# Decoder step on one core: token sums by VectorE instead of GpSimd, and an earlier index search with the later jobs planned behind it

## The chip, the cores and the metric

The kernel runs on one core of a Trainium2 chip. The metric is device time in microseconds for one launch; the time before is the median of three runs, and one more execution was taken by the hardware profiler. The engines are named as the profile names them: PE (TensorE, its matrix multiplications), PEld (TensorE, loading of stationary operands), DVE (VectorE), ACT (ScalarE), POOL (GpSimd) and SP (SyncE, which only issues DMAs here). Engines run their own queues in order, each with its waits, and meet through semaphores.

## The reference

One decoder layer on a prompt of 1024 tokens and on 8 sample sequences of one token each, all in float32. The token vector (2048 wide) is normalised, multiplied by one wide matrix, split into heads, and two branches are computed: sparse attention and an mLSTM. Their outputs are gated, concatenated and multiplied by an output matrix.

```
h = rmsnorm(x, norm_w); p = split(h @ w_in)
scores = sum_h relu(q_idx[h] . k_idx) * w_idx[h]      # "indexer", 16 heads of 64
idx = top_k(scores, 256)                              # causal, per query
o   = softmax(q . k[idx] * scale) . v[idx]            # 8 heads, 2 KV heads
C, n, m, h_ml = mlstm(mq, mk, mv, igate, fgate)       # chunks of 64
x   = x + concat(o * silu(az), norm(h_ml) * sigmoid(mo) * silu(mz)) @ w_out
y   = rmsnorm(x, final_norm_w)
```

For the 8 samples keys and values come from a paged cache of 4096 positions, are scored, the best 256 are selected, and the rows are gathered.

## The kernel before, in words

**Precision.** Every large float32 product is made of three matmuls: each operand is split into a high part (H, a cast by ACT) and a low part (L, the remainder, a subtraction by DVE), and H·H, H·L and L·H are added in PSUM. So each new operand costs one ACT and one DVE instruction before PE can use it. L256/L257 are such splits of weights, L1676/L1677 of token sums.

**Stages on PE.** (1) The projection: tiles t = 0 to 20 of 128 weight columns (L1547), in three chunks of 344 tokens, 144 matmuls a tile. (2) The gate stage: tiles 21 to 60, made with fewer products out of sums of weight blocks and sums of token blocks, in the manner of Strassen. Each product is 48 matmuls of 128x258 (L1729) into PSUM tiles `pj`. Its phases are: phase 0, 20 pairs of products, which in the order of product matmuls is from 2640 to 4560; phase 1, to 5520, with the token sum in slot 1; phase 3, to 6480, slot 0; phase 2, slot 2; and the rest to 9360. In phase 0 a fourth PSUM tile, `extra`, is taken out of the pool of 5 banks (`bank`) that the side jobs use for their matmuls. After each half product DVE evacuates PSUM with a combine (L1824). (3) The output projection (L2094).

**Token sums.** `job_prep` makes them in 16 steps: X (two halves of a token block, 128x516 each) is loaded through the DMA queue of POOL (L1402), multiplied by the norm weight (L1412) and by the reciprocal root mean square (L1413), four sums and differences are formed (L1418 to L1421), and the results are stored to `xsD` (L1422, L1423). X has 3 buffers, O (three sums) has 1; loads go out two steps ahead. In the gate stage `fill(slot, op)` puts eight loads of a sum into a list; each `tick`, once per half product, issues one of them, and three ticks later its split (L1676 on ACT, L1677 on DVE). `pin` keeps an instruction in the order in which it is written.

**Weight sums.** `job_usum` sums weight blocks by DMAs that add in memory (L1435, L1439).

**Side jobs.** All other work is written as generators that yield a weight, in three lanes. A job has a start and an end in tiles, and after every tile or half product `Lane.step` runs the lane's current job until its share of weight up to the end is used. Lane 0: gates, index, att, ml. Lane 1: prep, dscore, dsel, qrows, datt (which waits for the index to be done), dml. Lane 2: usum. `T_AK` is 9 and `T_G` is 21. A scheduler with a model of time then fixes each engine's queue from this order, the priorities and the pins.

**The index.** `job_index` treats query blocks in three groups of two. A load brings a quad (four heads of a query block; `qi`, L450, on ACT's queue). For each head PE makes the scores (L468), ACT applies relu (L470), DVE weights and adds them (L473). Then a binary search for the 256th score runs in steps of ACT sign counts (L517) and DVE counts (L543). For the samples `dscore` and `dsel` do the same: L1062, L1083, L1089 and L1079 on DVE, L1064 on PE, whose total L1087 reads. `datt` then gathers keys (L1294), forms logits on DVE (L1318, L1322), transposes (L1336), makes a softmax (L1341 to L1351, PE L1358, L1359), multiplies gathered values (L1372) and writes out (L1379). `att` does the prompt's attention: transposes L597, logits L634, L635 on DVE, exponentials L651 on ACT, transposes L678, values L687.

```
def step(self, now, amount=1.0):        # Lane
    self.now = now
    self.debt -= amount
    while self.debt < 0:
        ...
        self.debt += self._next()       # weight * (quarter tiles left to end) / weight left
```

## Time and profile before

| | before |
|---|---|
| median of 3 runs | 2004.84 us (2001.0 to 2009.59) |
| profiled execution | 1996.96 us |
| its span | 1995.2 us |
| mean granted PE clock | 0.976 |
| PE busy | 1903.5 us |
| DVE busy | 1391.9 us |
| ACT busy | 916.5 us |
| POOL busy | 516.5 us |
| moved by DMA | 474.46 MB |

The profiled execution lies 0.4% under the median of the runs. Times in the trace are counted from the start of the span. Product matmuls follow one another on PE, so their count is a clock of its own: product matmul 2640 ends at 518.5 us, 4560 at 784.5 us, 5520 at 976.5 us, 6480 at 1185.7 us, 9360 at 1644.2 us.

### The profile page before, as it was taken

How to read it: one execution, taken by the hardware profiler on the slowest of the kernel's cores; microseconds unless marked ns; L12 is line 12 of the kernel's file. 1: busy time of each engine (PE TensorE's matmuls, PEld its weight loads, DVE VectorE, ACT ScalarE, POOL GpSimd, SP SyncE). 2: the span in 40 equal slices, each digit the busy share in tenths (PEclk: the TensorE clock that was granted, in tenths of full speed). 3: DMA queues.
4: the chain of work that ended last, by engine and by line, in shares of the span. 5: the costliest groups of instructions: out<-in, count | busy, mean ns of one | idle time of the engine just before them, and what ended most of it. 6: DMA issues, size and time to landing. Idle time of an engine off the chain costs nothing. (4 is left out here: it accounts for less than half of the span.)

```text
span 1995.2 us, 37381 instructions
## 1 busy us (share of the span) xinstructions
PE 1903.5 (95%) x13422; PEld 1822.9 (91%) x13422; DVE 1391.9 (70%) x3261; ACT 916.5 (46%) x1826; POOL 516.5 (26%) x614
## 2 busy tenths in 40 slices
PE   9999989999999999995699999999999999999997
PEld 9999989999999999994599989999999999977876
DVE  8554245765698988976465656566897666788887
ACT  8222136345434466410355545545565434455645
POOL 0698921222111000034000111011112131106633
PEclk9999999999999999897799999999999999999999
DMA  7578674665998647597577999678898957898866
GB/s 258 172 217 242 210 205 143 196 178 160 312 311 259 181 149 238 184 336 256 128 198 226 290 290 277 181 223 270 299 331 294 224 198 255 273 344 285 291 207 221
DMA packets 252918, 474.46 MB, mean 238 GB/s; under 512 B 40549, under 2 KB 116133, under 8 KB 246333
## 3 DMA queue, kind: packets, MB, share of 16 engines
q1 hardware_dynamic: 217261, 356.70, 54.6%
q0 software_dynamic: 21504, 107.32, 21.2%
q10 hardware_dynamic: 13968, 8.06, 1.4%
q8 instruction: 105, 1.72, 0.3%
q14 instruction: 80, 0.66, 0.1%
HBM read 381.54 MB, written 174.32 MB: 279 GB/s over the span
## 5 line engine op out<-in xcount | busy, mean ns | idle before, releaser
L1729 PE MATMUL pj<-xH 128*128 128x258 f32 x1920 | 545.5, 286 | 6.1 <-ACT xH L1676 2.8
L1729 PE MATMUL pj<-xL,xH 128*128 128x258 f32 x1920 | 547.0, 285 | 0.3 <-DVE xL L1677 0.2
L1729 PE MATMUL pj<-xH,xL 128*128 128x258 f32 x1920 | 545.9, 285 | 0.0
L1729 PEld LDWEIGHTS pj<-xH 128*128 128x128 f32 x1920 | 363.9, 190 | 9.5 <-ACT xH L1676 3.8
L1729 PEld LDWEIGHTS pj<-xL,xH 128*128 128x128 f32 x1920 | 365.6, 190 | 2.5 <-DVE xL L1677 0.9
L1729 PEld LDWEIGHTS pj<-xH,xL 128*128 128x128 f32 x1920 | 365.4, 191 | 1.5
L1547 PE MATMUL pj<-xH,wH 128*128 128x344 f32 (+1 forms) x816 | 265.4, 328 | 0.9 <-DVE mfull L379 0.5
L1547 PE MATMUL pj<-xL,wH 128*128 128x344 f32 (+1 forms) x816 | 265.0, 325 | 0.0
L1547 PE MATMUL pj<-xH,wL 128*128 128x344 f32 (+1 forms) x816 | 264.8, 325 | 0.0
L1439 POOL DMA_DIRECT2D usD<-in_wa_dram x80 | 65.9, 892 | 604.4 <-DMA usD<-in_wa_dram 367.9
L257 DVE TENSOR_TENSOR wL<-wraw,wH 128x512 fp32r<-128x512 f32 (+2 forms) x151 | 116.8, 784 | 120.5 <-ACT wH L256 111.3
L256 ACT CAST wH<-wraw 128x512 fp32r<-128x512 f32 (+2 forms) x151 | 90.0, 608 | 216.9 <-PE pj L1547 151.4
L1547 PEld LDWEIGHTS pj<-xH,wH 128*128 128x128 f32 x816 | 153.8, 189 | 2.1 <-ACT xH L313 0.9
L1547 PEld LDWEIGHTS pj<-xL,wH 128*128 128x128 f32 x816 | 154.0, 189 | 0.8 <-DVE xL L314 0.3
L1547 PEld LDWEIGHTS pj<-xH,wL 128*128 128x128 f32 x816 | 154.0, 189 | 0.3
L2094 PE MATMUL pj<-wH,sH 128*128 128x512 f32 x336 | 131.0, 390 | 0.7 <-ACT wH L2078 0.4
L2094 PE MATMUL pj<-wL,sH 128*128 128x512 f32 x336 | 125.9, 392 | 5.3 <-DVE wL L2083 5.0
L2094 PE MATMUL pj<-wH,sL 128*128 128x512 f32 x336 | 130.7, 389 | 0.0
L470 ACT ACTIVATE rl<-bank 128x512 f32<-128x512 f32 (+2 forms) x160 | 79.1, 522 | 90.7 <-PE bank L468 50.7
L473 DVE SCALAR_TENSOR_TENSOR s<-rl,wiN,s 128x512 f32<-128x512 f32 (+2 forms) x150 | 95.0, 653 | 31.7 <-ACT rl L470 29.5
L1729 PE MATMUL bank<-xL,xH 128*128 128x258 f32 x320 | 91.4, 286 | 0.0
L1729 PE MATMUL bank<-xH,xL 128*128 128x258 f32 x320 | 91.3, 285 | 0.0
(487 smaller groups left out, 4466.7 us busy)
## 6 DMA issues: line engine op xcount, KB each, us to landing
usD<-in_wa_dram POOLq DMA_DIRECT2D x80, 512.0 KB, 8.0
wraw<-in_wt_dram SPq DMA_DIRECT2D x144, 256.0 KB
usD<-in_wa_dram SPq DMA_DIRECT2D x40, 512.0 KB
usD<-usD POOLq DMA_DIRECT2D x40, 512.0 KB, 7.2
wraw<-in_wa_dram SPq DMA_DIRECT2D x78, 256.0 KB
wraw<-in_wo_dram SPq DMA_DIRECT2D x64, 256.0 KB
ev<-spD SPq DMA_DIRECT2D x62, 258.0 KB
spD<-ev SPq DMA_DIRECT2D x60, 258.0 KB
```

What stands on the lines that cost most here:

```text
L256: a = SC.copy(H[:, s, :cols], raw[:, s, :cols])
L257: return a, V.tensor_tensor(L[:, s, :cols], raw[:, s, :cols], H[:, s, :cols].bitcast(F32), OP.subtract)
L470: SC.activation(r[:, :cn], p[:, :cn], AF.Relu)
L473: v = V.scalar_tensor_tensor(s[:, c0:c0 + cn], r[:, :cn], wv, s[:, c0:c0 + cn], OP.mult, OP.add)
L1439: pin(G.dma_start(usD[n, i], src, accum_op=OP.add, max_dma_last_dim=8192))
L1547: m = PE.matmul(ps[:cols, :cn], w_[:, k, :cols], x_[kk][:, c0:c0 + cn], start=(kk == ends[0] and z == 0), stop=(kk == ends[1] and z == 2))
L1729: PE.matmul(ps[c], w_[:, q, ks], x[y][:, c * CS:c * CS + CS], start=(first and q == 0 and k == 0 and z == 0), stop=(q == 1 and k == 3 and ...
L2094: PE.matmul(ps[b], S_[x][:, b * 128:b * 128 + 128], T_[y], start=(k == 0 and z == 0), stop=(k == 7 and z == 2))
```

## The change

1. *Token sums.* The multiplications by weight and by rms become one fused DVE instruction for each half (two a step), and the four POOL sums become three DVE instructions, the first of which makes two sums at once. The order of the sums in `xsD` changes, and with it the numbers in `fill`. The DMAs stay on POOL's queue.
2. *Index.* `qi` has 3 buffers, three quads are loaded at the start and after each search, later loads are two quads ahead. The job stands from tile 9.6 to 26.5 (12.3 to 30 before).
3. *Plan.* The start and end of prep, dscore, dsel, qrows, datt, att, ml, dml and usum are moved.
4. *Gate stage.* The slot splits are written at high priority, and the fill of slot 1 starts 20 half products into phase 0 instead of 40.

```diff
@@ job_index
-                    qis[n] = px.tile([128, 4, 128], F32R, name="qi", bufs=2)
+                    qis[n] = px.tile([128, 4, 128], F32R, name="qi", bufs=3)
...
-            load_q(0)
-            load_q(1)
+            for n in range(3):
+                load_q(n)
...
-                            if nq + 1 < len(quads) and (nq + 1) % 8 > 1:
-                                load_q(nq + 1)
+                            if (nq + 2) % 8 > 2:
+                                load_q(nq + 2)
...
-                load_q(nq)
-                load_q(nq + 1)
+                for z in range(3):
+                    load_q(nq + z)
@@ job_prep
-                a11, a21, a12, a22 = (X[:, y, h] for y in range(2) for h in range(2))
                 for y in (1, 0):
-                    w = nw[:, k + 8 * y:k + 8 * y + 1].unsqueeze(2).to_broadcast([128, 2, CS])
-                    pin(G.tensor_tensor(X[:, y], X[:, y], w, OP.mult))
-                    pin(G.tensor_tensor(X[:, y], X[:, y], halves[:, :, c:c + CS], OP.mult))
+                    pin(V.scalar_tensor_tensor(X[:, y], X[:, y], nw[:, k + 8 * y:k + 8 * y + 1], halves[:, :, c:c + CS],
+                                               OP.mult, OP.mult))
...
-                pin(G.tensor_tensor(O[:, 0], a21, a22, OP.subtract))
-                pin(G.tensor_tensor(O[:, 2], a11, a21, OP.subtract))
-                pin(G.tensor_tensor(O[:, 1], O[:, 0], a11, OP.subtract))
-                pin(G.tensor_tensor(a12, a12, O[:, 1], OP.add))
+                pin(V.tensor_tensor(O[:, 0:2], X[:, 0], X[:, :, 1], OP.subtract))
+                pin(V.tensor_tensor(O[:, 2], O[:, 1], X[:, 0, 0], OP.subtract))
+                pin(V.tensor_tensor(X[:, 1, 0], X[:, 1, 0], O[:, 2], OP.add))
@@ lanes
-                   Job("index", T_AK + 3.3, 30, ...),
-                   Job("att", T_G, 45.0, ...),
-                   Job("ml", T_G + 20, 56.6, ...)]),
-             Lane([Job("prep", 3, T_AK + 4.2, ...),
-                   Job("dscore", T_AK + 6, 21.0, ...),
-                   Job("dsel", T_AK, 28.5, ...),
-                   Job("qrows", T_G + 0.2, 29, ...),
-                   Job("datt", T_G + 4, 32.0, ...),
-                   Job("dml", T_G + 20, 54.5, ...)]),
-             Lane([Job("usum", T_AK + 3.4, 46.0, ...)])]
+                   Job("index", T_AK + 0.6, 26.5, ...),
+                   Job("att", T_G + 8, 44.5, ...),
+                   Job("ml", T_G + 20, 57.0, ...)]),
+             Lane([Job("prep", 3, T_AK + 2, ...),
+                   Job("dscore", T_AK + 3, 18.0, ...),
+                   Job("dsel", T_AK, 26.0, ...),
+                   Job("qrows", T_G + 0.2, 27, ...),
+                   Job("datt", T_G + 7.5, 32.5, ...),
+                   Job("dml", T_G + 20, 55.0, ...)]),
+             Lane([Job("usum", T_AK + 3.0, 46.0, ...)])]
@@ gate_stage
-                pin(SC.copy(h, l.bitcast(F32)))
-                pin(V.tensor_tensor(l, l.bitcast(F32), h.bitcast(F32), OP.subtract))
+                with tc.high_priority():
+                    pin(SC.copy(h, l.bitcast(F32)))
+                    pin(V.tensor_tensor(l, l.bitcast(F32), h.bitcast(F32), OP.subtract))
...
-        fills += [None] * (NP * 2)
-        fill(1, 3)
+        fills += [None] * NP
+        fill(1, 4)
...
-        fill(0, 4)
+        fill(0, 2)
...
-        fill(1, 2)
+        fill(1, 3)
```

In the changed file lines behind 1424 are numbered 2 or 3 lower: L1729 becomes L1727, L1824 becomes L1822, L1713 and L1718 (splits of weights for the products) become L1711 and L1716. Three places of the engines' order show what moves.

PE at the end of phase 1, before: the rows are the last matmuls of phase 1 (L1729), then those of `datt` and `att`.

```order
L1729 MATMUL pj_5145<-xL,xH 128x258
L1729 MATMUL pj_5145<-xH,xL 128x258
L1336 MATMUL bank<-cst,lT 64x128
L1338 MATMUL bank<-onesf,kn 64x1
L1336 MATMUL bank<-cst,lT 64x128
L1358 MATMUL bank<-cst,jk 128x64 x2
L1359 MATMUL bank<-cst,pb 128x64
L1372 MATMUL bank<-cv,PZ 32x256 x16
L1379 MATMUL bank<-cst,jk 128x128 x4
L597 MATMUL bank<-cst,pP 128x128 x8
L634 MATMUL bank<-xH,qH 128x512
```

They stand together behind product matmul 5520; the first matmul of phase 3 follows only after L634 and L678. In the changed kernel the same matmuls stand among those of phase 1. The first of them, on PE, behind product matmul 5059:

```order
L1727 MATMUL pj_5635<-xH 128x258
L1336 MATMUL bank<-cst,lT 64x128
L1338 MATMUL bank<-onesf,kn 64x1
L1727 MATMUL pj_5635<-xL,xH 128x258
L1727 MATMUL pj_5635<-xH,xL 128x258
L1727 MATMUL pj_5635<-xH 128x258
L1727 MATMUL pj_5635<-xL,xH 128x258
L1727 MATMUL pj_5635<-xH,xL 128x258
L1336 MATMUL bank<-cst,lT 64x128
L1727 MATMUL pj_5633<-xH 128x258
```

The others follow at product matmuls 5108 (L1358), 5149 to 5282 (L1372), 5308 (L1379), 5432 (L597) and 5458 (L634). The index's first score (L468) stands at product matmul 1056, where before it stood at 1452, and its last at 2933, before at 3937.

PE in the changed kernel in phase 0, behind product matmul 2808 (its row comes first): a run of index scores (L468) and of dsel's totals (L1064), of which rows are left out in two places.

```order
L1727 MATMUL pj_5635<-xH,xL 128x258
L468 MATMUL bank<-ki_1987,qi 128x384
L468 MATMUL bank<-ki_1988,qi 128x384
L468 MATMUL bank<-ki_1987,qi 128x512
L468 MATMUL bank<-ki_1988,qi 128x512
...
L1064 LDWEIGHTS onesb
L1064 MATMUL bank<-cb,onesb 128x24
L468 MATMUL bank<-ki_1987,qi 128x512
L468 MATMUL bank<-ki_1988,qi 128x512
...
L1727 MATMUL bank<-xH 128x258
```

In all 58 matmuls L468 and four L1064 stand there without a product between; before, they lay between products. The matmul that follows writes `extra`, in a PSUM bank that a total of dsel had last.

DVE in the changed kernel, early in the projection: the fused passes (L1410) and sums (L1416 to L1418) of prep stand in DVE's queue between its other work.

```order
L257 TENSOR_TENSOR wL<-wraw,wH 128x512
L1410 SCALAR_TENSOR_TENSOR X<-X,nw,rstd 128x516
L1417 TENSOR_TENSOR O<-O,X 128x258
L1410 SCALAR_TENSOR_TENSOR X<-X,nw,rstd 128x516
L1418 TENSOR_TENSOR X<-X,O 128x258
L257 TENSOR_TENSOR wL<-wraw,wH 128x512
L379 TENSOR_TENSOR iqe<-pj_791,rstd 128x388
L1416 TENSOR_TENSOR O<-X 128x516
```

Before, none of them was on DVE; L257 splits projection weights and L379 evacuates projection tiles.

22 lines of the change are left out of this document (11 added, 11 removed).

## The prediction

> **What bounds the kernel now.** I read the page first: one core, and TensorE (PE) is the engine that counts.
>
> ```profile
> span 1995.2 us, 37381 instructions
> PE 1903.5 (95%) x13422; PEld 1822.9 (91%) x13422; DVE 1391.9 (70%) x3261; ACT 916.5 (46%) x1826; POOL 516.5 (26%) x614
> PE   9999989999999999995699999999999999999997
> PEclk9999999999999999897799999999999999999999
> ```
>
> PE is busy 95% of the span, and busy hides half-speed time, so the room is where a PE digit or a clock digit falls: slices 19 and 20 (about 898 to 998 us) and, less, slice 17. The waits of PE name what it stood for, and the stretches around them give the price.
>
> ```profile
> PE bank L1336 <- issue: 10.3, 1, 10.3
> PE bank L597 <- DMA bias<-biasS: 9.4, 1, 9.4
> PE bank L468 <- DMA qi<-qS: 8.0, 2, 7.7
> PE bank L1372 <- DMA cv<-in_cv_dram,ixv: 7.5, 5, 3.0
> PE bank L1152 <- DVE oa L1146: 3.1, 1, 3.1
> ```
>
> (line waited for: us in all, times, longest.) Then the windows; the columns are the window, its length, busy time and instructions of PE, PEld, DVE, ACT and POOL, the granted clock, the DMA share and GB/s.
>
> ```profile
> 68.00:255.00 187.00, 187.00 (x1120) 186.08 (x1119) 82.52 (x120) 36.30 (x62) 175.46 (x194) 1.00 0.78 227
> 255.00:272.00 17.00, 10.20 (x64) 9.87 (x62) 6.42 (x13) 3.77 (x8) 3.43 (x5) 0.91 1.01 285
> 272.00:282.00 10.00, 8.81 (x45) 8.59 (x46) 3.71 (x6) 3.05 (x7) 1.30 (x2) 0.81 0.85 237
> 791.00:805.00 14.00, 8.22 (x37) 6.74 (x38) 13.23 (x43) 7.63 (x14) 0.00 (x0) 0.63 0.49 177
> 805.00:812.00 7.00, 7.00 (x48) 7.00 (x48) 5.68 (x16) 3.51 (x6) 0.00 (x0) 0.76 0.78 271
> 874.00:882.00 8.00, 6.20 (x40) 6.00 (x39) 7.32 (x10) 0.91 (x2) 3.59 (x3) 0.79 1.04 395
> 916.20:976.50 60.30, 21.48 (x74) 10.31 (x74) 22.94 (x60) 6.48 (x17) 17.73 (x20) 0.60 0.79 213
> 976.50:983.00 6.50, 6.49 (x26) 5.92 (x27) 5.04 (x11) 2.68 (x5) 0.00 (x0) 0.54 0.11 33
> ```
>
> From 916.2 to 976.5 us nothing is the bound: PE 21.5 of 60.3 us busy, DVE 22.9, ACT 6.5, POOL 17.7. It is one chain of latencies, and PE has no large product in it:
>
> ```profile
> 915.78 0.29 PE L1729 MATMUL pj<-xL,xH 128*128 128x258 f32 x1
> 915.90 0.28 PE L1729 MATMUL pj<-xH,xL 128*128 128x258 f32 x1
> 926.48 0.39 PE L1336 MATMUL bank<-cst,lT 128*64 128x128 f32 x1 [10.29 <-issue]
> 960.30 1.09 PE L597 MATMUL bank<-cst,pP 128*128 128x128 f32 x4 [9.42 <-DMA bias<-biasS]
> 976.51 1.01 PE L1729 MATMUL pj<-xH 128*128 128x258 f32 x3 [0.55 <-ACT xH L1676]
> 976.49 0.70 DVE L1677 TENSOR_TENSOR xL<-xL,xH 128x516 fp32r<-128x516 f32 x1
> ```
>
> The next product needs a split operand, and its split (L1676/L1677) stands on ACT and DVE behind the work of datt and att; so 60 us of small work ran with no product between. (The first two rows also give the pace of a product: 0.12 us a matmul.) This, not the VectorE share, is what the change can move most.
>
> **The change part by part.** The sum is made on the profiled execution, 1996.96 us, of which the span is 1995.2. The median of the runs is 2004.84 us, 0.4% above; I add the difference at the end.
>
> *The cluster.* In the changed order the same matmuls of datt and the first of att stand among the products of phase 1 (first L1336 after product matmul 5059 instead of 5520), and the slot splits carry a higher priority. What goes: 60.3 less the PE work in it at full clock, 21.48 × 0.60 = 12.9, is 47.4 us; behind it 6.5 × (1 − 0.54) = 3.0 us of slow clock; 50.4 together. What stays: each link of the chain must now be covered by products placed between the links, and the order puts them with little to spare. The nearest row for a link whose data was already under way is that of the cv gathers, 7.5 us over five waits: between nothing and the whole of it I leave 4. Gain 46 (43 to 50).
>
> *Five slot splits at the start of phase 1.* The stretch 791–805 loses 14 − 8.22 × 0.63 = 8.8 us, and 805–812 loses 7 × 0.24 = 1.7: 10.5. The split operands of that slot now stand 26 to 36 evacuations earlier, since the fill begins 20 half products sooner. Gain 10.5; below, 5, because dsel's L1152 waits in there too (3.1).
>
> *The third query buffer.* The load of a quad of query heads went out only when its buffer came free:
>
> ```profile
> 258.19 0.37 ACTq L450 DMA_DIRECT2D qi<-qS  x1
> 273.25 0.87 ACT L470 ACTIVATE rl<-bank 128x384 f32<-128x384 f32 x2 [8.17 <-DMA qi<-qS]
> ```
>
> It took up to 15 us, and PE lost 17 − 10.20 × 0.91 = 7.7 and then 10 − 8.81 × 0.81 = 2.9 us in the two windows from 255 to 282: 10.6. Now the third load goes out with the first two, and each later one is two quads ahead instead of one. The index's 24 quads and its searches are planned over 16.9 tiles; a tile of 144 matmuls takes some 24 us (187 / 1120 each, first window), so a quad has 17 us, and two quads ahead cover 15, unless quads bunch. Gain 8 (4 to 10.6).
>
> *The token sums on VectorE.* 128 GpSimd operations go, 80 DVE ones come.
>
> ```profile
> L1413 POOL TENSOR_TENSOR X<-X,rstd 128x516 f32<-128x516 f32 x32 | 42.1, 1315 | 2.5
> L1412 POOL TENSOR_TENSOR X<-X,nw 128x516 f32<-128x516 f32 x32 | 39.2, 1226 | 0.7 <-DVE iqe L379 0.3
> L1779 DVE SCALAR_TENSOR_TENSOR ev<-ev 128x516 f32<-128x516 f32 x16 | 11.0, 690 | 2.4 <-ACT ev L1755 2.4
> L1824 DVE TENSOR_TENSOR ev<-pj,ev 128x258 f32<-128x258 f32 x123 | 51.5, 422 | 33.3 <-PE pj L1729 32.7
> X<-in_xT_dram POOLq DMA_DIRECT2D x32, 258.0 KB, 4.6
> xsD<-O POOLq DMA_DIRECT2D x16, 387.0 KB, 5.0
> ```
>
> By the shapes, a step is 3 × 0.69 + 2 × 0.42 = 2.9 us on DVE, 16 steps 47 us. The work that hides it is PE's own: from 68 to 255 us PE never stops and DVE is busy 82.5 of 187 us. If DVE were full there, all 47 would show; it would be at 130 of 187, so I count it at nothing. There is even relief. The weight splits slow down while POOL computes:
>
> ```profile
> 68.00:260.00 192.00, 38.78 (x39) 1.00 0.78 228
> 260.00:516.00 256.00, 20.67 (x30) 0.99 0.64 183
> ```
>
> (L257 alone, DVE busy and count): 0.99 us each against 0.69 later, so 12 us of DVE come back. What is new is that an in-order DVE waits for a load that POOL's queue issues; two steps ahead is some 16 us against a landing of 4.6, so only the first steps can wait: +2 us (0 to 10). The three sums' new order in memory and the two renamed fills cost nothing: same bytes, same queue.
>
> *The index earlier, and the new place where it meets dsel.* The searches move into the projection, where DVE has room. But in the changed order, at product matmul 2808 (phase 0, tile 21), 58 L468 and four L1064 stand in a row on PE with no product between; the next product writes the PSUM bank whose last reader is dsel's L1087 on DVE. Between DVE's last evacuation before and that L1087 stand 19 L473 of 512, 11 of 384, four each of L1083 and L1062 and a dozen L1089 and L1079 each:
>
> ```profile
> L473 DVE SCALAR_TENSOR_TENSOR s<-rl,wiN,s 128x512 f32<-128x512 f32 x75 | 55.5, 746 | 12.0 <-ACT rl L470 11.0
> L473 DVE SCALAR_TENSOR_TENSOR s<-rl,wiN,s 128x384 f32<-128x384 f32 x45 | 27.6, 614 | 19.5 <-ACT rl L470 18.5
> L1083 DVE TENSOR_TENSOR ri<-sp,im 128x792 bf16<-128x792 f32 x15 | 14.7, 979 | 0.1
> L1062 DVE TENSOR_REDUCE cb<-ri 128x24 bf16<-128x792 bf16 x15 | 14.5, 968 | 0.0
> L1089 DVE COPY_PREDICATED im<-im 128x8 int32<-128x8 int32 x46 | 7.7, 167 | 0.6
> 600.00:710.00 110.00, 35.83 (x128) 20.86 (x128) 1.00 0.75 210
> ```
>
> 19 × 0.746 + 11 × 0.614 + 4 × 0.979 + 4 × 0.968 + 24 × 0.167 = 32.7 us, 34 with the single small ones. PE has in that time 24 product matmuls (2.9 us) and 58 of L468 at 0.28 (last row, L468 alone on PE): 16.2. So PE idles some 14 us, the totals counted, and if the clock falls as it did behind the cluster (3.0), the loss is 17. It can be nothing if DVE has run ahead, or 34 + 3 = 37 if PE finds nothing to do at all. I take 17. The Trainium skill, "TensorE: Matmul & The Clock Gate", Part 1 ("What's actually happening"), has the clock fall only after an idle window of about 3.4 us; the trace disagrees in part, since the clock stood at 0.63 from 791 to 805 us, where PE's longest wait is 3.1 us. By that rule a burst cut into short gaps by L468 would cost 14 instead of 17.
>
> Jobs that only move (att, ml, dml, usum, dsel) keep PE's work the same, and nothing waits on them now that stands in the waits above; zero, within 4 either way. The 8 − 6.20 × 0.79 = 3.1 us lost from 874 to 882, in datt's first DVE work, I let stay.
>
> Sum: −46 − 10.5 − 8 + 2 + 17 = −45.5: 1951.5 on the profiled execution, 1959 on the median's basis (2004.84 − 45.5 = 1959.3).
>
> **The rivals.**
>
> *R1, the burst is hidden.* DVE has caught up by 2808, or the bank is free: −62 instead of −45.5, 1942 us. For: in the part of the kernel now emptied of index work DVE has slack. Against: the rows stand in order, and 14 us of extra DVE work is not made up in a stretch that is DVE-heavy already.
>
> *R2, the stall only moves.* datt comes 461 matmuls × 0.12 = 55 us earlier on PE. If its inputs (the gathers after dsel, the index's end) don't, PE waits at the new places for as long; the gain is 10.5 + 8 − 17 − 2, about nothing: 2005 us. For: the gathers, POOL's, follow dsel, and dsel shares DVE with the index and now the token sums. Against: the index's last score stands 1004 matmuls earlier (2933 instead of 3937), about 120 us of products; in evacuations its end is 32 earlier; at 24 matmuls each that is some 92 us, still 37 more than datt needs.
>
> *R3, slower: VectorE waits in line.* DVE takes its queue in order, so a token sum whose load or whose single O buffer is not there holds the evacuations and weight splits behind it. If each of the 16 steps waits out a landing of 4.6 to 5.0 us, that is 80 us on DVE with 47 of work; in 68–255 us DVE has 104 idle, so 23 us at least, and up to 80, since a weight split is due every few us, come out on PE, and the slower start carries datt with it (R2): 2005 + 23 = 2028 us. It decides from the point at which a step waits longer than PE's stock of split weights lasts, a few us. Against: loads are issued two steps ahead. The Trainium skill's page "SBUF — State Buffer", section "SBUF: two separate sides", has an exclusive port lock between the two engines and says that transfers issued from GpSimd's queue can starve while DVE holds it: a rule against this change, which leaves the loads there. The trace shows the lock's direction (0.99 against 0.69 us) but no starved transfer; by it the time would be R3's.
>
> **How the numbers follow.** Forecast as summed 0.57, R1 0.17, R2 0.13, R3 0.08, other mishaps of planning 0.05. The likeliest gives 1959 us. Its own terms spread it to 1940–1980 (burst 0 to 37, cluster 43 to 50, the rest ±5). With R1 and part of R2 taken in, the range is 1931 to 1992; R3 and the worse half of R2 lie outside. About 0.5%, 10 us, is what a measurement of this kernel can tell from no change. Faster: forecast, R1 and a part of R2, 0.80. Same: most of R2, 0.11. Slower: R3 and the rest, 0.09.
>
> **What would show it.** Right: no stretch of tens of us around the first L1336 with PE under half busy; slices 19 and 20 at 9 in PE and clock; no PE wait for qi over 3 us; L257 near 0.7 us before 260 us; POOL near idle until the sums; a dip in PE of 10 to 20 us in phase 0 with L473 and L1087 as releasers. Wrong: PE waiting for ck, cv or lT at the new places (R2); DVE idle before the fused passes with X or O as releaser and PE waiting for wL (R3). My burst term is the least certain; if the dip is absent the time should be near 1942.

## The result: 11 us faster, a quarter of what was forecast

| | before | changed |
|---|---|---|
| median | 2000.76 us (17 runs, 1996.95 to 2009.84) | 1989.8 us (17 runs, 1983.97 to 2000.09) |
| ratio to before | | 0.9944, 95% interval 0.9926 to 0.9961 |
| profiled execution | 1996.96 us | 1999.2 us |
| its span | 1995.2 us | 1997.4 us |

The change gains 8 to 15 us. The forecast was 1959 us, a gain of 45.5; the measured time lies in its range, but at the far end, and the likeliest case did not come. One warning for what follows: the profiled execution of the changed kernel is near the slow end of its runs and that of before next to its fastest, so the changed kernel's span is 2.2 us longer than that of before, though its median is 11 us lower. The traces tell where time was lost and won; the 11 us are told by the medians.

The page of the changed kernel, in the lines shown of before:

```profile
span 1997.4 us, 37376 instructions
PE 1910.9 (96%) x13422; PEld 1829.6 (92%) x13422; DVE 1406.6 (70%) x3341; ACT 918.6 (46%) x1826; POOL 388.6 (19%) x486
PE   9979999999979999889999999999999999999997
PEclk9989999999989999998999999999999999999999
```

The hole of before, 5 and 6 in slices 19 and 20, is gone. In its place stand three shallower ones: slice 3 (100 to 150 us, in the projection), slice 12 (549 to 599 us, the start of phase 0), and slices 17 to 19 (799 to 949 us, phase 1). The windows around them, columns as in the prediction, before and then changed:

```profile
93.90:151.00 57.10, 57.10 (x325) 56.78 (x324) 31.04 (x44) 13.37 (x23) 55.06 (x63) 1.00 0.77 229
547.00:603.00 56.00, 56.00 (x470) 55.71 (x468) 51.79 (x153) 19.67 (x32) 10.58 (x15) 1.00 1.04 307
790.00:860.00 70.00, 64.10 (x492) 62.41 (x491) 62.95 (x148) 31.88 (x49) 0.78 (x1) 0.90 0.69 222
```

```profile
93.90:151.00 57.10, 46.49 (x242) 45.83 (x241) 31.31 (x62) 10.36 (x18) 17.69 (x24) 0.91 0.74 220
547.00:603.00 56.00, 42.99 (x224) 34.66 (x223) 51.21 (x116) 29.79 (x54) 5.50 (x8) 0.91 0.61 164
790.00:860.00 70.00, 58.97 (x460) 58.01 (x459) 36.64 (x51) 13.19 (x18) 20.58 (x22) 0.95 1.03 350
976.60:1036.50 59.90, 59.14 (x464) 57.34 (x463) 40.87 (x102) 34.39 (x76) 4.81 (x6) 1.00 0.76 221
```

A loss is taken as in the prediction: the length less PE's busy time at the granted clock. So the first stretch loses 57.1 − 46.49 × 0.91 = 14.8 us where before lost none, and the second 56.0 − 42.99 × 0.91 = 16.9. The third is the one to remember: in the 70 us ahead of datt's work the transfers took a share of 1.03 (350 GB/s), where before it was 0.69. The last row is the place where before had its cluster: phase 3 now starts without a hole.

Worked out in the same manner from PE's records between given product matmuls, the losses by stage are (us of the profiled executions). A count stands for the moment at which the next product matmul begins: the 976.5 us given for 5520 of before are the first matmul of phase 3, behind the cluster, and the last of phase 1 had ended at 916.2.

| stage (product matmuls) | before | changed | forecast of the difference | measured |
|---|---|---|---|---|
| projection (0 to 2640) | 13.4 | 21.0 | −6 | +7.6 |
| phase 0 (2640 to 4560) | 0.6 | 20.1 | +17 | +19.5 |
| phase 1 and the step into phase 3 (4560 to 5760) | 66.0 | 33.0 | −56.5 | −33.0 |
| phase 3 to 7440 | 6.8 | 7.5 | 0 | +0.7 |
| 7440 to 9360 | 5.0 | 5.3 | 0 | +0.3 |
| 9360 to the last matmul of the output projection | 12.5 | 15.6 | 0 | +3.1 |

They add up to 104.3 us before and 102.5 after. (By these sums the span would be 1.8 us shorter; it is 2.2 longer. The 4.0 us between, 0.2% of the span, are in no wait: PE's busy time is 7.4 us longer for the same 13422 matmuls, of which half speed accounts for 2.9.) So two rows hold the miss: 23.5 us in phase 1 and 13.6 in the projection. The waits of PE in the changed kernel say which links these are:

```profile
PE pj L1727 <- DVE ev L1822: 20.8, 9, 5.0
PE pj L1544 <- DVE iqe L379: 11.4, 3, 6.1
PE bank L1064 <- DVE cb L1062: 6.5, 2, 4.8
PE bank L468 <- DMA ki<-kS: 3.6, 2, 2.1
```

No wait for qi is left (8.0 us before), and none of L1336 (10.3) or L597 (9.4) either. New are products that wait for an evacuation with a combine (L1822), projection tiles that wait for theirs (L379), dsel's totals behind DVE, and the index's first scores, which at their earlier place wait for keys.

**The projection.** DVE's waits from 60 to 270 us, and the groups of DVE with shapes kept apart:

```profile
DVE X L1410 <- DMA X<-in_xT_dram: 22.5, 13, 3.1
DVE O L1416 <- DMA xsD<-O: 18.8, 10, 5.2
```

```profile
L257 DVE TENSOR_TENSOR wL<-wraw,wH 128x512 fp32r<-128x512 f32 x145 | 101.4, 711 | 53.8 <-ACT wH L256 52.1
L1410 DVE SCALAR_TENSOR_TENSOR X<-X,nw,rstd 128x516 f32<-128x516 f32 x32 | 23.6, 750 | 22.5 <-DMA X<-in_xT_dram 22.5
L1416 DVE TENSOR_TENSOR O<-X 128x516 f32<-128x516 f32 x16 | 11.1, 691 | 18.8 <-DMA xsD<-O 18.8
```

The passes cost about what was estimated (750 and 691 ns against 690), and weight splits run at 711 ns on the mean; from 68 to 260 us they take 686 (22.6 us for 33), where beside GpSimd they took 994. But DVE stood 41 us in its own line, not for the first steps only: 13 times for the load of X, 10 times for the store that frees the only O. The plan runs a step about every 9 us; a load, the passes and a store through three X and one O need about as long. The evacuation L379, queued behind, is what PE then waits for.

**Phase 0.** PE's rows at the burst:

```profile
584.52 0.20 PE L1064 MATMUL bank<-cb,onesb 128*128 128x24 bf16 x1 [4.85 <-DVE cb L1062]
...
588.13 0.42 PE L1727 MATMUL bank<-xH 128*128 128x258 f32 x1
588.34 0.42 PE L1727 MATMUL bank<-xL,xH 128*128 128x258 f32 x1
```

The first product to write `extra` comes right behind the totals, and for the first products the pace is 0.21 us instead of 0.12: the clock is at half. Between product matmuls 2760 and 2880 the loss is 13.0 idle and 4.1 slow, 17.1 us; forecast was 17.

**Phase 1.** The transfers most waited for, by DVE from 815 to 977 us and by ACT from 760 to 880 us, and POOL's issues of weight sums (L1432 copies, L1436 adds) and the first gather (L1294):

```profile
DVE ev L1822 <- DMA ev<-spD: 11.3, 4, 4.8
```

```profile
ACT xH L1710 <- DMA wL<-usD: 16.8, 2, 11.0
```

```profile
643.84 0.52 POOL L1432 DMA_DIRECT2D usD<-usD  x1 [4.75 <-DMA usD<-in_wa_dram]
782.35 1.56 POOL L1436 DMA_DIRECT2D usD<-in_wa_dram  x2 [137.99 <-DMA usD<-in_wa_dram]
...
809.06 1.81 POOL L1294 DMA_INDIRECT ck<-in_ck_dram,idxs  x1 [0.31 <-PE bank L1727]
```

The index is done 76 us sooner (its last L561 at 779.9 us instead of 855.6), as the prediction had it. But the first gather follows it by 29 us where before it was 10, datt's first L1318 comes at 830.7 (874.6 before) and its last at 889.3 (926.4), and att's first L634 at 964.9, where before it was at 963.9. Of 76 us nothing reaches att. But PE doesn't wait for datt or att here: the longest wait at one of their matmuls is 1.3 us, and L634 stands in PE's line behind product matmul 5458. What PE waits for in phase 1 are the evacuations of its products (L1822); and ahead of these DVE itself waits, as the two rows show, for reloads of partial results and, through ACT, for the weights to be split (L1710). On the way, between 644 and 782 us, POOL issued no weight sum; those it had left fall on the stretch in which the gathers, the reloads of partial results (`ev<-spD`) and the weights of phase 1 (`wL<-usD`) are wanted. The bytes moved show it: the two windows 520 to 790 and 790 to 980 us, before and then changed:

```profile
DMA packets 32345, 63.67 MB, mean 236 GB/s; under 512 B 5180, under 2 KB 18236, under 8 KB 30605
DMA packets 21961, 47.34 MB, mean 249 GB/s; under 512 B 6325, under 2 KB 7733, under 8 KB 21146
```

```profile
DMA packets 29249, 50.69 MB, mean 188 GB/s; under 512 B 6687, under 2 KB 18143, under 8 KB 28164
DMA packets 21931, 57.31 MB, mean 302 GB/s; under 512 B 4463, under 2 KB 5679, under 8 KB 20575
```

13 MB fewer in the first, 10 MB more in the second; of the 10, POOL's queue has 5.3 (14.78 MB instead of 9.44). What POOL waited for in these 138 us the profile calls `usD<-in_wa_dram`. That is the name of its own adds, but also of the base copies that SP issues for the sums (L1432), and by the trace's semaphores it was one of the latter: SP issued it at 774.6 us, it landed at 781.8, and POOL went on at 782.4. Why that add waits for so late a copy, when by the order in the program the copy for its own block went out at 667.0 us, isn't established.

### The profile page after: what moved, and what is told of

It reads as the page before. It is cut to its first block, busy times and chain, and to the rows that moved or that the text cites. A ratio compares the mean times of both kernels' runs of the same rounds, so it can differ in the third digit from the quotient of the medians.

```text
span 1997.4 us, 37376 instructions
## 1 busy us (share of the span) xinstructions
PE 1910.9 (96%) x13422; PEld 1829.6 (92%) x13422; DVE 1406.6 (70%) x3341; ACT 918.6 (46%) x1826; POOL 388.6 (19%) x486
## 5 line engine op out<-in xcount | busy, mean ns | idle before, releaser
L1727 PE MATMUL pj<-xH 128*128 128x258 f32 x1920 | 550.1, 288 | 21.5 <-DVE ev L1822 20.8
L1727 PE MATMUL pj<-xH,xL 128*128 128x258 f32 x1920 | 550.1, 287 | 1.7 <-issue 1.7
L1727 PE MATMUL pj<-xL,xH 128*128 128x258 f32 x1920 | 548.8, 286 | 0.8 <-issue 0.7
L1727 PEld LDWEIGHTS pj<-xH 128*128 128x128 f32 x1920 | 366.9, 191 | 26.2 <-DVE ev L1822 20.3
L1727 PEld LDWEIGHTS pj<-xH,xL 128*128 128x128 f32 x1920 | 367.7, 192 | 3.5 <-issue 2.5
L1727 PEld LDWEIGHTS pj<-xL,xH 128*128 128x128 f32 x1920 | 367.6, 191 | 2.1 <-issue 0.6
L1436 POOL DMA_DIRECT2D usD<-in_wa_dram x80 | 66.3, 927 | 615.8 <-DMA usD<-in_wa_dram 392.6
L1544 PEld LDWEIGHTS pj<-xH,wH 128*128 128x128 f32 x816 | 154.7, 190 | 14.4 <-DVE iqe L379 12.3
L257 DVE TENSOR_TENSOR wL<-wraw,wH 128x512 fp32r<-128x512 f32 (+2 forms) x151 | 103.7, 700 | 54.9 <-ACT wH L256 53.1
L470 ACT ACTIVATE rl<-bank 128x512 f32<-128x512 f32 (+2 forms) x160 | 79.8, 522 | 77.9 <-DVE s L473 30.6
L468 PE MATMUL bank<-ki,qi 128*128 128x512 f32 (+2 forms) x320 | 82.3, 378 | 10.0 <-ACT rl L470 4.1
L1710 ACT CAST xH<-wL 128x1024 fp32r<-128x1024 f32 x46 | 48.2, 1049 | 94.5 <-PE pj L1727 37.6
```

Source lines behind the costliest of these rows:

```text
L257: return a, V.tensor_tensor(L[:, s, :cols], raw[:, s, :cols], H[:, s, :cols].bitcast(F32), OP.subtract)
L468: PE.matmul(p[:, :cn], qi[:, h % 4, :], ki[x][:, c0:c0 + cn], start=(x == 0), stop=(x == 1))
L470: SC.activation(r[:, :cn], p[:, :cn], AF.Relu)
L1436: pin(G.dma_start(usD[n, i], src, accum_op=OP.add, max_dma_last_dim=8192))
L1544: m = PE.matmul(ps[:cols, :cn], w_[:, k, :cols], x_[kk][:, c0:c0 + cn], start=(kk == ends[0] and z == 0), stop=(kk == ends[1] and z == 2))
L1710: SC.copy(H, raw[2])
```

## The experiments

Twelve kernels, each timed against before in three rounds, all but one edits of the changed kernel (the fourth is an edit of before). Before's own median was 2000.76 us beside the changed kernel, 2001.8 beside e1 to e4, 2005.06 beside e5 to e7, 2003.29 beside e8 to e10 and 2001.13 beside e11 and e12, so kernels of different groups are better compared by their ratios than by their medians. "Phase 1 loss" is the loss from product matmul 4560 to 5760 of the profiled execution.

| | edit | median us | ratio to before (95%) | phase 1 loss |
|---|---|---|---|---|
| before | | 2000.76 | | 66.0 |
| changed | | 1989.8 | 0.9944 (0.9926 to 0.9961) | 33.0 |
| e1 | bank of `extra` taken early | 1997.65 | 0.9994 (0.9973 to 1.0015) | 57.1 |
| e2 | token sums back on GpSimd | 1990.8 | 0.9955 (0.9932 to 0.9977) | 20.5 |
| e3 | token sums spread | 1992.35 | 0.9947 (0.9922 to 0.9971) | 30.6 |
| e4 | before with part 4 alone | 2008.88 | 1.0027 (1.0004 to 1.005) | 80.3 |
| e5 | e1, weight sums of phase 3 left out | 1987.46 | 0.9926 (0.9899 to 0.9953) | 50.4 |
| e6 | e1, weight sums end sooner | 1976.44 | 0.9871 (0.9825 to 0.9916) | 36.0 |
| e7 | e1 and e2 together | 2014.66 | 1.0036 (1.0012 to 1.006) | 61.8 |
| e8 | weight sums end sooner, alone | 1998.27 | 0.9971 (0.9953 to 0.9988) | 34.8 |
| e9 | e6, slot 2 filled later | 1984.03 | 0.989 (0.9859 to 0.9922) | 37.4 |
| e10 | e9 and e3 together | 1982.14 | 0.9887 (0.9853 to 0.9921) | 37.6 |
| e11 | e10, weight sums split in two jobs | 1978.68 | 0.9894 (0.9854 to 0.9935) | 18.7 |
| e12 | weight sums split, alone | 1984.73 | 0.9912 (0.988 to 0.9944) | 5.0 |

**e1: is the burst there for want of a bank?** `extra` is taken out of the pool one tile ahead of the gate stage, before the totals of dsel can have its bank.

```diff
+    extras = []
...
+        if t == T_G - 2:
+            extras.append(bank())
+            with tc.high_priority():
+                V.memset(extras[0][:, :CS], 0.0)
...
-        extra = bank()[:, :CS]
+        extra = extras.pop()[:, :CS]
```

> The changed kernel, with the fourth PSUM tile of phase 0 (extra) claimed one tile before the gate stage by a small high-priority write of zeros on DVE; nothing is left out. Theory 1, the run of 58 index matmuls at product matmul 2808 is one wait for a PSUM bank that the side jobs' backlog keeps taking: the run is gone from PE, the 13.0 us of idle and 4.1 us of slow clock in product matmuls 2760 to 2880 fall to under 4, and the time falls by 13 to 17 us against the changed kernel (1989.8 to about 1975). Rival, the backlog of some 34 us on DVE is the cause and only shows there: the same loss comes back within the next 1000 product matmuls, and the time stays at 1985 to 1992.

Measured: 1997.65 us, slower than the changed kernel (the intervals of the two ratios don't meet). The burst is gone, and product matmul 4560 is reached at 793.3 us instead of 815.1. Then all of it is given back, and more. Windows of e1: the place of the burst, and two in phase 1.

```profile
547.30:568.50 21.20, 20.62 (x153) 19.70 (x152) 18.76 (x43) 11.03 (x20) 3.65 (x5) 1.00 1.01 313
810.70:858.00 47.30, 34.16 (x242) 33.75 (x242) 11.16 (x18) 5.95 (x7) 10.10 (x11) 0.80 0.99 342
949.30:1037.80 88.50, 71.10 (x492) 65.79 (x491) 46.87 (x120) 39.31 (x87) 7.97 (x10) 0.87 0.69 187
```

From 811 to 858 us PE loses 20 us at a transfer share of 0.99, and DVE, nearly idle, waits 20.4 us for three reloads of partial results (`ev<-spD`); from 949 us a cluster is back (27 us). datt is where it was (att's first L634 at 967.8 us, 964.9 in the changed kernel), so products that come 22 us sooner only run out 22 us sooner. The burst's mechanism is shown; its 17 us as a term of the sum are not, since taking them away brought nothing.

**e2: what do the token sums on VectorE bring?** The six GpSimd operations of before stand in `job_prep` again, with the new order of the sums.

```diff
...
-                    pin(V.scalar_tensor_tensor(X[:, y], X[:, y], nw[...], halves[...], OP.mult, OP.mult))
...
+                    pin(G.tensor_tensor(X[:, y], X[:, y], w, OP.mult))
+                    pin(G.tensor_tensor(X[:, y], X[:, y], halves[:, :, c:c + CS], OP.mult))
...
-                pin(V.tensor_tensor(O[:, 0:2], X[:, 0], X[:, :, 1], OP.subtract))
-                pin(V.tensor_tensor(O[:, 2], O[:, 1], X[:, 0, 0], OP.subtract))
-                pin(V.tensor_tensor(X[:, 1, 0], X[:, 1, 0], O[:, 2], OP.add))
+                pin(G.tensor_tensor(O[:, 1], a21, a22, OP.subtract))
+                pin(G.tensor_tensor(O[:, 0], a11, a21, OP.subtract))
+                pin(G.tensor_tensor(O[:, 2], O[:, 1], a11, OP.subtract))
+                pin(G.tensor_tensor(a12, a12, O[:, 2], OP.add))
```

> The changed kernel with part 1 undone: the token sums' 8 operations a step are on GpSimd again, in the new order of the sums; index, plan and gate stage as changed. Theory 1, VectorE waits in its queue for each step's load and store, and that costs the 10.6 us of PE idle and 3.8 us of slow clock in product matmuls 480 to 720: both fall to about nothing, the fused passes' only gain (L257 0.69 instead of 0.99 us) is off the path, so the time falls by 10 to 16 us to 1974 to 1980. Rival, the sums on VectorE are what makes room (GpSimd holds VectorE up when both run): the time rises above 1995.

Measured: 1990.8 us, the same time as the changed kernel. The loss between product matmuls 480 and 720 falls from 14.4 us to nothing, but POOL's queue now holds back what stands behind the sums: the gathers of dscore and the weight sums. Windows of e2, the projection and dscore's place, and PE's longest wait from 220 to 390 us:

```profile
93.20:135.80 42.60, 42.60 (x243) 42.48 (x242) 19.90 (x29) 9.86 (x17) 40.74 (x45) 1.00 0.77 227
232.30:282.20 49.90, 40.93 (x241) 40.35 (x241) 33.44 (x89) 27.43 (x71) 27.25 (x30) 0.90 0.49 153
```

```profile
PE bank L1028 <- DMA usD<-in_wa_dram: 9.7, 1, 9.7
```

12.0 us are lost from 1200 to 1440 and 14.3 from 1560 to 1800. So the sums' 14.4 us on DVE are real, and with this plan GpSimd costs as much, later; neither of the two times expected came. The weight splits (L257) are back at 1008 ns from 68 to 260 us (34.3 us for 34).

**e3: is it the pace of the token sums?** Same passes on DVE, given 4.2 − 2 = 2.2 tiles more, and dscore moved behind.

```diff
-             Lane([Job("prep", 3, T_AK + 2, 1 + 16 * 2, job_prep),
-                   Job("dscore", T_AK + 3, 18.0, 24 + 128 + 2, job_dscore),
+             Lane([Job("prep", 3, T_AK + 4.2, 1 + 16 * 2, job_prep),
+                   Job("dscore", T_AK + 4.8, 18.0, 24 + 128 + 2, job_dscore),
```

> The changed kernel with the token sums on VectorE, but planned to end at tile 13.2 as before instead of 11 (and dscore to start at 13.8), so that a step comes every 11 to 12 us instead of every 9. Theory 1, the loss early in the projection is VectorE waiting for the load and the store of a step, which take some 9 us one behind the other with three X buffers and one O: with steps further apart than that, the waits of L1410 and L1416 (22.5 and 18.8 us) fall to under 10 each and PE's loss in product matmuls 480 to 720 from 14.4 to under 5 us; time 1978 to 1984. Rival, it is the 47 us of added work, or the first steps alone: the loss stays at 10 or more and the time at 1987 to 1992.

Measured: 1992.35 us, again no change. The stretch is clean, and the waits of DVE show why. A window of e3 and DVE's waits there:

```profile
97.00:139.50 42.50, 42.50 (x243) 42.50 (x242) 24.56 (x50) 10.10 (x18) 13.25 (x18) 1.00 0.79 229
```

```profile
DVE O L1416 <- DMA xsD<-O: 16.3, 4, 5.5
DVE X L1410 <- DMA X<-in_xT_dram: 4.5, 3, 2.7
```

Loads are waited for 4.5 us instead of 22.5 and the store of O still 16.3, yet PE loses nothing here. The time expected, 1978 to 1984, didn't come: what was won is lost again in small pieces, 4.9 us before 480, 3.6 from 720 to 960, 6.1 from 1560 to 1800, 3.7 from 2040 to 2640, and 15.9 from 5760 to 6480 against 3.6 (the burst is smaller, 13.0). att's first L634 comes at 938.0 us, 27 sooner than in the changed kernel, and that doesn't show in the time either.

**e4: is the cluster the plan's work or the gate stage's?** Before, with part 4 of the change alone.

```diff
+                with tc.high_priority():
+                    pin(SC.copy(h, l.bitcast(F32)))
+                    pin(V.tensor_tensor(l, l.bitcast(F32), h.bitcast(F32), OP.subtract))
...
-        fills += [None] * (NP * 2)
+        fills += [None] * NP
```

> The kernel before with part 4 of the change alone: slot splits at high priority and the fill of slot 1 begun 20 half products into phase 0. Theory 1, the cluster of datt and att at product matmul 5520 comes from the plan (index and datt late), not from the splits' priority: the 60 us with no product stay, and only the losses around the slot-1 splits at 791 to 812 us go, 8 to 11 us: 1990 to 1993. Rival, the splits' place in the queues makes the cluster: it dissolves, and the time falls by 40 us or more, to 1960.

Measured: 2008.88 us, slower than before by 1 to 10 us, where one theory had 1990 to 1993 and the other 1960. Windows of e4, the first part of phase 1 and the cluster, and PE's longest waits:

```profile
799.70:906.00 106.30, 102.08 (x848) 101.13 (x847) 88.33 (x192) 36.42 (x52) 15.88 (x14) 1.00 0.83 256
906.00:1029.60 123.60, 59.87 (x346) 46.90 (x345) 64.35 (x138) 31.29 (x72) 30.37 (x32) 0.67 0.59 161
```

```profile
PE bank L1336 <- issue: 25.1, 1, 25.1
PE bank L634 <- ACT qH L617: 12.0, 1, 12.0
```

The 11.0 us of the slot splits are won (the last product of phase 1 ends 9.9 us sooner), and the cluster grows from 51.5 to 76.1 us. Of these 25 us, 10 are that gain, waited out, since datt doesn't come sooner; the rest is the chain itself, which comes later in this execution (first L1336 at 931.4 us instead of 926.5, first L634 at 979.3 instead of 963.9), and it is the slowest of e4's ten. The splits' term is right as a loss and worth nothing alone. And part 4 alone doesn't dissolve the cluster.

**e5: do the weight sums crowd phase 1?** e1 with the weight sums of phase 3 left out: phase 3 takes a plain block in their place, so what this kernel computes is no longer the layer.

```diff
-        for n, src in ((3, None), (2, 1)):
+        for n, src in ((2, 1),):
...
+            if kind == 3:
+                return A["wa"][T_G + 2 * i, 1].rearrange("p q a b -> p q (a b)")
...
-             Lane([Job("usum", T_AK + 3.0, 46.0, 8 * NP, job_usum)])]
+             Lane([Job("usum", T_AK + 3.0, 29.0, 4 * NP, job_usum), Job("usum2", 38, 46.0, 2 * NP, job_usum2)])]
```

> Kernel of e1_claim_bank with the weight sums of phase 3 left out (20 copies and 20 adding transfers; phase 3 multiplies by a plain weight block instead, so its result is another), the sums of phase 1 at the same pace and those of phase 2 from tile 38 to 46. It empties product matmuls 4560 to 5760 (about 790 to 1040 us) of most weight-sum traffic and leaves PE, DVE and ACT work as it is. Theory 2, phase 1 is bound by the transfers (DMA share 0.9 to 1.03 in e1 and in the changed kernel), which delay partial results, splits and datt's gathers: PE's idle and slow clock in product matmuls 4560 to 5760, 57 us in e1, falls to under 30, and the time by 20 us or more against e1 (1998 to under 1978). Rival, datt's chain is slow by its own latencies and its place in DVE's queue: the loss stays at 45 or more and the time within 8 us of e1.

Measured: 1987.46 us, 10 us less than e1 (14 by the ratios), but not the fall that was expected of the phase. Windows of e5: the gathers, the stretch behind them, the cluster.

```profile
808.70:855.70 47.00, 32.67 (x243) 32.27 (x242) 12.65 (x21) 5.95 (x7) 11.26 (x12) 0.82 0.92 300
855.70:913.20 57.50, 57.50 (x483) 57.50 (x482) 53.06 (x66) 11.28 (x14) 17.81 (x15) 1.00 0.82 270
929.80:1003.80 74.00, 50.81 (x308) 42.04 (x307) 31.49 (x79) 25.56 (x55) 18.09 (x26) 0.77 0.78 219
```

The second stretch lost 12.3 us in e1 and loses nothing here. The first still loses 20 and the cluster some 35, since the sums of phase 1 itself still fall together with the gathers and datt isn't sooner (att's first L634 at 960.8 us). The theory as I had worded it, with a phase under 30 us, fell (50.4); that bytes taken away help the stretch that they stood in held.

**e6, e8: the weight sums sooner,** with e1's edit and without it.

```diff
-             Lane([Job("usum", T_AK + 3.0, 46.0, 8 * NP, job_usum)])]
+             Lane([Job("usum", T_AK + 3.0, 40.0, 8 * NP, job_usum)])]
```

> Kernel of e1_claim_bank with the weight sums planned to end at tile 40 instead of 46, so that more of them are made between 550 and 780 us, where the DMA share is 0.5 to 0.6; complete. Theory 2: part of the saturated traffic moves out of phase 1, the loss in product matmuls 4560 to 5760 falls from 57 to 35 to 45 us, time 1980 to 1988. Rival (the chain's own latencies, or the sums are late for another reason): the loss stays, 1993 to 2000.

> The changed kernel with one number changed: the weight sums end at tile 40 instead of 46; extra is not claimed early. Theory 3, the last weight sums of phase 1 crowd into 782 to 822 us in the changed kernel, on GpSimd's queue ahead of datt's gathers and in the transfers; made earlier they leave that place, and phase 1 (product matmuls 4560 to 5760) loses under 20 us instead of 32, with the burst at 2808 still there (17 us): about 1978 to 1984. Rival, the early claim of the bank is what made e6 fast, together with the sums: alone it gives 1988 to 1992, as the changed kernel.

Measured: e6 1976.44 us, the fastest of all and under the 1980 to 1988 expected, and its interval lies wholly below that of the changed kernel; e8 1998.27, no faster than the changed kernel. In e6 the cluster is down to 6.2 us and 4920 to 5400 loses nothing; only the stretch of the gathers still loses:

```profile
808.50:867.00 58.50, 35.87 (x243) 35.19 (x242) 32.86 (x53) 5.96 (x7) 19.08 (x18) 0.77 0.98 303
```

(58.5 − 35.87 × 0.77 = 31 us.) One number, 46 to 40, is worth 21 us on top of e1 (25 by the ratios) and nothing, if not a loss, on top of the changed kernel. In e8 the burst is still there, and the phase loses 34.8 us, as much as without the edit (33.0) and not the under 20 expected, though the gathers go at 788 us, 21 sooner than in the changed kernel, and att's first L634 comes at 932.3, 33 sooner. The last sum of phase 1 is issued there at 642 us; now seven adds for phase 3 go out at 777 to 780 us, right ahead of phase 1.

**e7: do two gains add?** e1 and e2 in one kernel; the two edits are shown above.

> Both single undoings together: extra claimed early as in e1, token sums on GpSimd as in e2. If losses ahead of phase 1 added up, 17 us of the burst and 10 or more of the projection, it would be 1965 or less. Theory 2: whatever is won ahead of phase 1 is given back in it, because the end of datt's chain and the transfers hold att to about 960 us whenever phase 1 begins; 1985 to 1998, with a larger cluster at product matmul 5520.

Measured: 2014.66 us, slower than either (1997.65 and 1990.8) and than before. Neither of the times expected came. Phase 1 loses 61.8 us, 28 of them at the cluster and 34 ahead of it, and att's first L634 is at 987.5 us, 20 later than in e1 and not at about 960: the index ends at 805.9 us, 14 later than in e1, and datt behind it.

**e9, e10: is it the loads of slot 2?** e6 with the fill of slot 2 moved 32 half products later, and this with e3's spread token sums.

```diff
         fill(0, 2)
+        fills += [None] * 32
         fill(2, 1)
```

> Kernel of e6_sums_sooner with the eight loads of slot 2 (needed in phase 2) put 32 half products later, out of the start of phase 1. Theory 3, the three waits of 7 to 9 us for partial results at 818 to 848 us in e6 (22.6 us idle and 7.2 slow in product matmuls 4680 to 4920) come from transfers crowding there, of which these are 2 of some 15 MB: they fall to half, time 1960 to 1970 against 1976. Rival, they come from the ring of four buffers for partial results or from the gathers: the loss in 4680 to 4920 stays over 22 us and the time at 1972 to 1980.

> Kernel of e9_slot2_later with the token sums spread to tile 13.2 as in e3. If the 14 us that VectorE's waits cost at product matmuls 480 to 720 are now free of the give-back in phase 1, the time falls by 8 to 14 us against e9; if datt's chain still sets the start of att, it falls by under 4 us, and phase 1 shows a longer wait.

Measured: 1984.03 and 1982.14 us, both by their ratios within each other's and e6's intervals; e9 lies above both ranges expected of it. From 4680 to 4920 e9 loses 28.8 us (e6 29.8) and e10 29.8: the loads of slot 2 were not it. From 480 to 720 e10 loses nothing, where e9 loses 14.2, but its median is only 2 us lower; the 8 to 14 us didn't come, and phase 1 loses no more than in e9. In e10, from 4680 to 4920, a window, ACT's longest wait, and POOL's row:

```profile
807.40:866.00 58.60, 32.81 (x242) 32.40 (x241) 31.68 (x48) 5.44 (x6) 17.73 (x18) 0.77 1.01 300
```

```profile
ACT xH L1710 <- DMA wH<-usD: 22.7, 1, 22.7
```

```profile
798.03 5.60 POOL L1436 DMA_DIRECT2D usD<-in_wa_dram  x7 [186.25 <-issue]
```

Seven adds of 512 KB go out together after POOL has stood for 186 us, the gathers go right behind them (the first at 806.85 us), and ACT then waits 22.7 us for a load of weights that phase 1 needs. This is the theory that the last two kernels test.

**e11, e12: the sums out of the way.** The weight sums of phase 1 end by tile 26; those of phases 3 and 2 become a job of their own behind datt. e11 has this on top of e10, e12 alone on top of the changed kernel.

```diff
...
-             Lane([Job("usum", T_AK + 3.0, 46.0, 8 * NP, job_usum)])]
+             Lane([Job("usum", T_AK + 3.0, 26.0, 4 * NP, lambda: job_usum(False)),
+                   Job("usum2", 33.5, 44.0, 4 * NP, lambda: job_usum(True))])]
```

> Kernel of e10_spread_and_later with the weight sums in two pieces: those of phase 1 end at tile 26, those of phases 3 and 2 begin at tile 33.5, so that none falls into the start of phase 1 (in e10 seven adding transfers start within 4 us at about 797 us, and the next weights come some 20 us late); complete. Theory 3, transfers crowding there cost the 25.8 us of idle and 4.0 of slow clock in product matmuls 4680 to 4920: these fall to under 12 together, time 1960 to 1972 against 1982. Rival, the ring of partial results or datt's gathers do: the loss stays at 25 or more and the time at 1978 or above.

> The changed kernel with only the weight sums split as in e11; the bank is not claimed early, the token sums are as changed. Theory 3: the loss of phase 1 (product matmuls 4560 to 5760, 33 us in the changed kernel) falls under 20 and the time to 1974 to 1982. Rival, the start of phase 1 is crowded by more than the sums, and what is won there is lost elsewhere: 1986 to 1998, as e8.

Measured: e11 1978.68 us, e12 1984.73. First a window of e11 in the place of the gathers, then the stretch behind; and e12's phase 1 and what follows:

```profile
808.00:836.70 28.70, 28.70 (x242) 28.70 (x241) 26.42 (x32) 5.44 (x6) 11.23 (x11) 1.00 1.03 390
933.00:1173.00 240.00, 217.03 (x1660) 211.71 (x1659) 138.32 (x369) 118.69 (x284) 28.06 (x39) 0.94 0.91 251
```

```profile
819.30:984.30 165.00, 161.76 (x1265) 154.25 (x1266) 109.02 (x229) 62.90 (x123) 28.34 (x27) 0.99 0.80 258
1035.00:1194.00 159.00, 148.85 (x1160) 146.03 (x1159) 89.41 (x241) 75.38 (x181) 22.00 (x33) 0.96 0.97 275
```

In e11 the 29.8 us are gone: PE never stops from 808 to 836.7 us although the transfers run at 390 GB/s, and none of POOL's adds is among them. The gathers go 10 us behind the index, and att's first L634 comes at 910.9 us, 54 sooner than in the changed kernel. In e12 phase 1 falls from 33.0 to 5.0 us. POOL's queue (q0; packets, MB, share of the 16 engines' time) from 790 to 980 us, in the changed kernel and in e12:

```profile
q0 software_dynamic: 3021, 14.78, 31.8%
q0 software_dynamic: 2016, 7.34, 15.2%
```

The queue of the other engines' transfers (q1) moves the same in both, 42.31 and 42.22 MB; and from 790 to 860 us the two kernels even move the same in all, 24.49 and 24.30 MB. So what costs is not the bytes of the stretch but that POOL's part of the weight sums is among them. That a later datt isn't what costs, e8 shows, with datt sooner and the loss still there. The cause of phase 1's loss is shown.

But of 28 us the median of e12 keeps 5 (6 by the ratios; its interval and the changed kernel's overlap), short of the time that I had put down. And e11's median is 3 or 4 us under e10's, but its ratio to before is no lower, so no gain is shown there, though phase 1 loses 19 us less; the 1960 to 1972 expected didn't come. The sums put off fall on phases 3 and 2, whose start had the transfers at 0.76 in the changed kernel and has them at 0.91 to 0.97 here. In e12 product matmuls 5760 to 6480 lose 15.0 us (3.6 in the changed kernel), in e11 18.8, with 10.1 more up to 7440. And e12's projection, in which the sums of phase 1 are made faster, loses 29.8 us instead of 21.0; no run shows why.

## Why the prediction was right and wrong, step by step

**The cluster (46, 43 to 50).** Right in its mechanism, wrong in "What stays", for which I left 4 us. The cluster fell from 51.5 to 0.8 us at its old place; e4 shows that part 4 alone doesn't do it and e2 that it goes without part 1, so the earlier index and the plan, which no run separates, did. But from product matmul 4920 on 21.7 us are lost, where before had 3.5 up to the cluster. I had priced the links by the waits for cv in a stretch of before with transfers at 0.79; now datt's gathers start in one at 1.03.

**"Jobs that only move … zero, within 4 either way".** This is the step that failed, and the one above fails by it. I followed a moved job by its matmuls on PE and by the waits that it stood in before, not by its transfers. With index, dsel and datt moved, POOL issued the weight sums later: 13 MB left the stretch 520 to 790 us, 10 MB came into 790 to 980, and there PE's products waited for weights and partial results. e12 takes the weight sums out of the way and phase 1's loss goes from 33.0 to 5.0 us.

**Five slot splits (10.5).** The loss was there and goes (11.0 to nothing in e4); in the changed kernel 8.7 us stand at the same products again (4560 to 4680), with other causes behind them. And in e4 it was worth nothing alone, since the chain of datt ended where it had ended.

**Third query buffer (8, 4 to 10.6).** Right: 9.5 us lost there before, none now. The earlier start of the index, for which I had no term, costs 5.3 us between product matmuls 960 and 1200, of which the wait for keys, `ki<-kS`, is 3.6.

**Token sums (+2, 0 to 10).** Mis-sized: 14.4 us. Durations and relief were right; "only the first steps can wait" was not. I compared a landing of 4.6 us with 16 us of two steps ahead, and left out that X comes free only after the store, and O too. In e3, at a slower pace, the loss is gone. This is R3's mechanism (DVE waits in line, and evacuations behind it), at a price below its 23 us. Of the page that the prediction weighed there, the Trainium skill's "SBUF — State Buffer", section "SBUF: two separate sides", the direction is seen again (711 against 994 ns); its starving of GpSimd's transfers isn't: e3 has the same DVE passes and the same queue, and the waits for loads are 4.5 us instead of 22.5, so the pace decides.

**The burst (+17, 0 to 37).** Right, 17.1 us, idle 13.0 and slow 4.1. The Trainium skill's idle window of 3.4 us ("TensorE: Matmul & The Clock Gate", Part 1, "What's actually happening") would have made it 14 with only short gaps. The row at 584.5 us has a gap of 4.85, and the clock is at half from 582.7 to 589.5 us, as by that rule; but it was granted at 0.51 from 569.0 to 572.4 us too, where no gap of PE in the burst so far was over 1.6 us, so the trace agrees in part only, as it did in before. Yet as a term it didn't add: e1 removes it and is 8 us slower.

**R2, the stall only moves.** Given 0.13, its number was nearest, by another road: that is luck and not its mechanism. Its condition, that datt's inputs don't come earlier, did not hold: the index ended 76 us sooner, the first gather went 56 us sooner and the first L1336 ran at 891.8 us instead of 926.5, and PE waits at datt's new places for 0.4 us in all. Of the 56.5 us forecast for phase 1, 23.5 were lost in the products that stand between.

**The sum.** The terms were added as if each loss were PE's own. Up to phase 1 they are not where PE comes to the work of datt and att before it is done: in e1 it stands 6.8 us at L597 and 5.9 at L634, and most of its 22 us and all of e4's 10 were waited out there. In the changed kernel and e2, PE doesn't stand there (1.3 and 1.5 us at L634). So the like times of att's first L634 in before, changed, e1, e2 and e5 (960.1 to 967.8 us) are no fixed point: it came at 938.0 in e3, 932.3 in e8 and 906.4 in e12. Nor does it make the time by itself, for e3 and e8 are no faster than the changed kernel. On the loss basis the forecast was −45.5 and the traces −1.8; the medians say −11. The miss of the traces is 23.5 us in phase 1, 13.6 in the projection, 2.5 in phase 0 and 4.1 behind.

**What stays open.** Why POOL's sums waited 138 us in the changed kernel and 186 in e10 for copies that SP issued late (in e10 one landed at 796.5 us, the adds went at 798.0): no run settles it. Why the medians keep only a fifth of what phase 1 gains in e12 is seen as losses in the trace (phases 3 and 2, and the projection), but I didn't try to spread the late sums over these. And executions of one kernel differ by some ±8 us, so single traces carry less than the tables suggest.

## What to carry to other kernels

When a job is moved, list its transfers as well as its instructions, and those of every other job on the queues that it shares: megabytes by window and by queue, before and after, show what comes into a stretch, and in one at a transfer share near 1 links that were cheap may come late. Where the busiest engine would come to a long chain of latencies before it is done, a gain ahead of it is waited out; so find that chain's end first, and don't add terms on its two sides. For work moved onto an in-order engine, compare the whole cycle of its buffers (load, passes, store) with the pace of the plan, not one landing with the steps ahead.

## What the runs showed of the hardware

A 512 KB load was waited for up to 22.7 us (e10) and 20.1 us (e6) when the transfer share was near 1, yet at 1.03 and 390 GB/s PE lost nothing in e11: what counts is which transfers share the stretch. From 790 to 980 us of the changed kernel POOL's queue, the weight sums and gathers, took 31.8% of the engines' time for 14.78 MB and the other queues 61.1% for 42.31, 1.5 times as much for a megabyte (1.3 times in e12). The subtraction of 128x512 took, from 68 to 260 us, 994 ns in before and 1008 in e2 with GpSimd computing beside it, and 686 in the changed kernel without, 1.4 to 1.5 times as long. And behind 13 us of waits the products started at 0.21 us a matmul instead of 0.12, and were back at 0.12 after seven of them.
